# A hybrid gMLP / state-space block: first loads in smaller pieces, the norm weight loaded apart, the first product in k order, one product on the un-normalised input

## The chip, the cores and the metric

The kernel runs on one core of one Trainium2 chip. The metric is the time of one execution on the device, in microseconds (us), as the median of several runs. The engines named below are PE (TensorE, the matmuls), DVE (VectorE), ACT (ScalarE), POOL (GpSimd) and SP (SyncE, which here only issues transfers). Each engine works through its own list of instructions in order; an instruction that waits holds back everything behind it on that engine.

## The reference

One layer works on 512 tokens of 1024 channels, all in float32 (inputs and outputs). Cut to what matters here:

```python
xn   = rmsnorm(x, mix_norm_w)                       # x * rsqrt(mean(x^2)) * w
proj = xn @ w_in                                    # 1024 -> 9248 columns
g_a, g_b, za, z, xbc, dt_raw = split(proj)
y_a  = gmlp_mixer(za) @ w_proj_a
xbc  = silu(causal_dwconv(xbc, conv_w, conv_b))     # 4 taps; x, B, C channels
y_b  = ssd_scan(x, softplus(dt_raw + dt_bias), -exp(a_log), B, C) ... @ w_proj_b
h    = x + (sigmoid(g_a) * y_a + sigmoid(g_b) * y_b) @ w_out
h    = h + ConvGLU(rmsnorm(h))                      # 2816 wide, 3 taps
out  = rmsnorm(h)
```

The row factor rsqrt(mean(x^2)) of the first norm belongs to a token. A product of weights with x * w (without that factor) can therefore be multiplied by the factor afterwards, token by token.

## The kernel before, in words

**Tiles.** Activations lie with channels on the 128 partitions and the 512 tokens along the free axis: `xT0` to `xT7` are the eight tiles of x. To get float32 accuracy from the fast matmul type, every operand is split into a high part and a low part (`h` and `l` at the end of a name: `xw0h`, `xw0l`), and each product is three matmuls, hi·xh, hi·xl and lo·xh, each 128x128 by 128x512. `cols()` makes a pair of 128-column products (tiles `...p`, one PSUM bank each) from eight input tiles: the weights come in two k blocks of four tiles (`w0`, `w1`), and a pair is 48 matmuls. `weights()` loads a block (tag `wraw`, four buffers), ACT copies it to the high part and DVE subtracts to get the low part.

**Two versions of the input.** `xw` is x times the norm weight, without the row factor; it needs only `xT` and the norm weight. `xn` is the normalised input; it needs `rb`, the row factors in all partitions, which come from the squares of all x tiles (`xq`, token sums `xss` and the broadcast `rbp` on PE). The first two pairs, `B0` and `C0`, are made from `xw`, and `unnorm()` multiplies their results by `rb` afterwards (`B0u`, `C0u`); all later products of the projection use `xn`.

**Order of the stages on PE.** Thirteen small float32 matmuls on a tile of ones (`warm`), each of which shows as two records; then the pairs B0, C0 (with `xss`, the dt products `dtp` and `rbp` in the middle of C0), x0, x2, x4, x6, B2, C2, x8, x10, x12, x14, then the gMLP products, the z pairs, and the projections, up to the down projection `dn`. Four PSUM banks in two pairs take the results in turn: B0, x0, x4, B2, x8 and x12 use one pair of banks, C0, x2, x6, C2 and x10 the other. `conv()` reads a product straight out of its bank: one ACT pass and three DVE passes (widths 511, 510, 509); after the last of these the bank is free for the next pair but one.

**The chain of the time steps.** `dt_chain()` turns `dtp` into step sizes in five pieces, which are put between the stages at the places `CHAIN` gives. Its last pieces are the running sums `acp` (PE), their copy `ac_k` (ACT), the transposes `ach` (PE), and then `achs` and `eahs` (ACT), which are written to DRAM (`acum_d`, `ea_d`) and read back by `ssm_load()` as `s0bc` and so on; the first state-space steps begin with x8. `alog`, a 128x32 tile, is loaded on the POOL queue and exponentiated by ACT (an instruction of the first piece of that chain, which depends on nothing but its load).

**What sets the order.** PE's order follows the program for B0 and C0 by hand; everywhere else a list scheduler with a time model arranges the instructions of each engine when the kernel is built. So a change in one place can move instructions elsewhere.

Of the kernel before, what the change touches and what calls it, by code (L numbers as in the profile page):

```python
# [17 lines left out]
KD = D // P  # L18
# [10 lines left out]
R_MIX, R_GB, R_CB, R_NW, R_FN, R_FCB, R_FW, R_CW, R_FCW, R_D, R_LW, R_LB, R_ALL = 0, 8, 24, 48, 64, 72, 116, 124, 220, 352, 368, 376, 384  # L29
U_GA, U_GB, U_U, U_Z, U_XS, U_B, U_C = 0, 4, 8, 12, 20, 28, 30  # L30
# [3 lines left out]
def kernel(  # L34
# [6 lines left out]
    dve, act, pe, pool, sync = nc.vector, nc.scalar, nc.tensor, nc.gpsimd, nc.sync  # L41

    const = ctx.enter_context(tc.tile_pool(name="const", bufs=1))
# [6 lines left out]
    def T(name, dt=F32):  # L50
        return tp.tile([P, S], dt, tag="t", name=name)

    def PM(name):
        return pp.tile([P, S], F32, tag="mm", name=name, bufs=4)

    def PA(name):
        return pp.tile([P, S], F32, tag="aux", name=name, bufs=4)
# [4 lines left out]
    def f(t):  # L62
        return t.bitcast(F32)
# [10 lines left out]
    def weights(src, shape, name):  # L74

        pieces = [slice(None)]
        if ahead:
            raw = ahead.pop(0)
            pieces = [slice(0, 2), slice(2, 4)]
        else:  # L80
            raw = wp.tile(shape, F32, tag="wraw", name=name + "r", bufs=4)
            sync.dma_start(out=raw, in_=src)
        hi = wp.tile(shape, F32R, tag="whi", name=name + "h")
        lo = wp.tile(shape, F32R, tag="wlo", name=name + "l")
        for q in pieces:
            act.activation(out=hi[:, q], in_=raw[:, q], func=AF.Copy)
            dve.tensor_tensor(out=lo[:, q], in0=raw[:, q], in1=f(hi)[:, q], op=ALU.subtract)
        return hi, lo

    def cols(w, u, xs, name):  # L90

        K = len(xs)
        ps = [PM(f"{name}p{i}") for i in range(2)]
        nb = K // 4
        for kb in range(nb):
            hi, lo = weights(w[u, kb], [P, 4, 2 * P], f"{name}w{kb}")

            def mm(i, k, part):
                xh, xl = xs[4 * kb + k]
                c = slice(i * P, (i + 1) * P)  # L100
                if part == 0:
                    pe.matmul(ps[i], lhsT=hi[:, k, c], rhs=xh, start=(kb == 0 and k == 0), stop=False)  # L102
                    pe.matmul(ps[i], lhsT=hi[:, k, c], rhs=xl, start=False, stop=False)
                else:
                    pe.matmul(ps[i], lhsT=lo[:, k, c], rhs=xh, start=False, stop=(kb == nb - 1 and k == 3))  # L105

            if kb < nb - 1:
                order = [(i, k, part) for part in range(2) for k in range(4) for i in range(2)]
            else:
                order = [(i, k, part) for i in range(2) for part in range(2) for k in range(4)]  # L110
            for o in order:
                mm(*o)
            tick()
        return ps
# [4 lines left out]
    def defer(fn, n=1):  # L119
        later.append([n, fn])  # L120

    def tick():
        due = []
        for e in list(later):
            e[0] -= 1
            if e[0] <= 0:
                later.remove(e)
                due.append(e[1])
        for fn in due:
            fn()  # L130
# [4 lines left out]
    warm = PA("warm")  # L135
    for i in range(WARM):
        pe.matmul(warm[:, 0:P], lhsT=ones, rhs=ones, start=True, stop=True)  # L137
# [9 lines left out]

    one = const.tile([P, 1], F32, name="one")
    dve.memset(one, 1.0)
    pcol = const.tile([P, R_ALL], F32, name="pcol")  # L150
    act.dma_start(out=pcol, in_=cols_in)
    act.activation(out=one, in_=one, func=AF.Square)
    wdt = const.tile([P, KD, HEADS], F32, name="wdt")
    pool.dma_start(out=wdt, in_=wdt_in)
# [3 lines left out]
    pool.dma_start(out=alog, in_=alog_in[0].partition_broadcast(P))  # L158
    xT, ahead = [], []
    for k in range(KD):  # L160
        t = T(f"xT{k}")
        sync.dma_start(out=t, in_=xt_in[:, k, :])
        xT.append(t)
        if k % 4 == 0:
            raw = wp.tile([P, 4, 2 * P], F32, tag="wraw", name=f"first{k}", bufs=4)
            for q in range(0, 4, 2):
                sync.dma_start(out=raw[:, q:q + 2, :], in_=w_in[U_B, k // 4][:, q:q + 2, :])
            ahead.append(raw)

    def pc(r):  # L170
        return pcol[:, r:r + 1]


    def rstd(ssq, n, name):

        m = ssq.shape[-1]
        v = sm.tile([P, m], F32, tag="rsv", name=name + "v")
        dve.tensor_scalar(out=v, in0=ssq, scalar1=1.0 / n, scalar2=EPS, op0=ALU.mult, op1=ALU.add)  # L178
        r = sm.tile([P, m], F32, tag="rsr", name=name + "r")
        pool.tensor_tensor(out=r, in0=v, in1=mhalf[:, :m], op=ALU.pow)  # L180
        return r

    def token_sums(sq, name):

        ps = PA(name)
        n = sq.shape[-1] // P
        for c in range(n):
            pe.matmul(ps[:, c * P:(c + 1) * P], lhsT=sq[:, c * P:(c + 1) * P], rhs=ones, start=True, stop=True)  # L188
        return ps.rearrange("p (c t) -> p c t", t=P)[:, 0:n, 0]

    def bcast_tokens(r, name):

        ps = PA(name)
        n = r.shape[-1]
        for c in range(n):
            pe.matmul(ps[:, c * P:(c + 1) * P], lhsT=r[:, c:c + 1].to_broadcast([P, P]), rhs=ident,
                      start=True, stop=True)
        return ps[:, 0:n * P]


    xw = []
    for k in range(KD):
        h = T(f"xw{k}h", F32R)
        act.activation(out=h, in_=xT[k], func=AF.Copy, scale=pc(R_MIX + k))
        l = T(f"xw{k}l", F32R)
        dve.scalar_tensor_tensor(out=l, in0=xT[k], scalar=pc(R_MIX + k), in1=f(h), op0=ALU.mult, op1=ALU.subtract)
        xw.append((h, l))


# [1 line left out]
    for b in range(2):  # L211
        t = tp.tile([P, 4, P], F32R, tag="t", name=f"wdt{b}")
# [16 lines left out]
    xn = []  # L229
# [13 lines left out]
    def dt_product(b):  # L243
        for k in range(4 * b, 4 * b + 4):
            for i in range(2):
                pe.matmul(dtp, lhsT=wd2[b][:, k % 4, :], rhs=xw[k][i], start=(k == 0 and i == 0),
                          stop=(k == KD - 1 and i == 1))
# [71 lines left out]
    def conv(u, t, name):  # L319

        c = T(name)
        act.activation(out=c, in_=u, func=AF.Identity, scale=pc(R_CW + 72 + t), bias=pc(R_CB + t))
        for j in (1, 2, 3):
            dve.scalar_tensor_tensor(out=c[:, j:], in0=u[:, :S - j], scalar=pc(R_CW + 24 * (3 - j) + t),  # L324
                                     in1=c[:, j:], op0=ALU.mult, op1=ALU.add)
        act.activation(out=c, in_=c, func=AF.Silu)  # L326
        return c
# [130 lines left out]


    def conv_pair(u, ct, dst, i, name):  # L460
        ps = cols(w_in, u + i // 2, xn, name)
        for q in range(2):
            dst[i + q] = conv(ps[q], ct + i + q, f"{name}c{q}")

    with tc.manual_schedule(engines={mybir.EngineType.PE}):
        ps = cols(w_in, U_B, xw, "B0")

        def x_norm():
            r1 = rstd(token_sums(xacc, "xss"), D, "xr")
            dt_product(0)  # L470
            dt_product(1)
            act.copy(out=rb, in_=bcast_tokens(r1, "rbp"))
            us.extend(unnorm(ps[q], f"B0u{q}") for q in range(2))
            x_split()

        us = []
        defer(x_norm)
        psC = cols(w_in, U_C, xw, "C0")
# [22 lines left out]
    for b in range(2):  # L501
        ps = [PM(f"vp{b}{t}") for t in range(NT)]
# [12 lines left out]
        for t in range(NT):  # L515
# [19 lines left out]
    for i in range(0, 8, 2):  # L535
        ssm_step()
        ps = cols(w_in, U_U + i // 2, xn, f"u{i}")
        for q in range(2):
# [5 lines left out]
            for t in range(NT):  # L544
# [4 lines left out]
                                     in1=radd[b][:, gg:gg + P].unsqueeze(1).to_broadcast([P, NT, P]),  # L549
                                     op0=ALU.mult, op1=ALU.add)  # L550
# [43 lines left out]
    for i in range(0, 8, 2):  # L594
        ps = cols(wpa_in, i // 2, ya, f"pa{i}")
        for q in range(2):
            t = T(f"m{i + q}")
            act.copy(out=t, in_=ps[q])
            m.append(t)
    for i in range(0, 8, 2):  # L600
        for q in range(4):
            defer(lambda t=2 * i + q: y_split(t), 1 + q // 2)
        ps = cols(w_in, U_GA + i // 2, xn, f"ga{i}")
# [5 lines left out]
    for i in range(0, 8, 2):  # L609
        ps = cols(w_in, U_GB + i // 2, xn, f"gb{i}")  # L610
# [5 lines left out]
    for i in range(0, 8, 2):  # L616
        ps = cols(wpb_in, i // 2, yb, f"pb{i}")
# [8 lines left out]
    for i in range(0, 8, 2):  # L626
        ps = cols(wo_in, i // 2, ms, f"wo{i}")
        for q in range(2):
            k = i + q
            h = T(f"hT{k}")  # L630
# [53 lines left out]
    for i in range(NFF):  # L684
        ps = cols(wup_in, i, hs, f"up{i}")
# [53 lines left out]
T_BUFS = 74  # L739
XPOOL = (4, 6)  # L740
CHAIN = (1, 5, 9, 10)
WARM = 13


# [49 lines left out]
```

## Time and profile before

| what | value |
|---|---|
| time, median of 3 runs | 1041.57 us (1040.82 to 1041.67) |
| profiled execution, its own time | 1039.9 us |
| its span, first to last instruction | 1038.2 us |
| mean granted TensorE clock | 0.996 |
| PE busy | 1016.6 us (98%) |
| DVE / ACT / POOL busy | 616.6 (59%) / 451.2 (43%) / 52.6 (5%) us |
| bytes moved | 109.85 MB, mean 106 GB/s |

In a timeline row the first number is the start in us from the start of the span, the second the duration (of the whole group where the row ends in x2 or more), then engine, line, operation, the tile written, the arrow and the tiles read. What stands in brackets is idle time of the engine just ahead of the row, and what ended it. DMA rows give the tile, the queue that issued, the size and the time from issue to landing.

### The profile page before, as it was taken

The numbers are of one execution on the slowest core, as the hardware profiler recorded it, in microseconds if no ns is written. First come the engines' busy times: TensorE is split into PE (matmuls) and PEld (weight loads), VectorE is DVE, ScalarE is ACT, GpSimd is POOL, SyncE is SP. The second block draws the span as 40 slices with busy tenths as digits, with TensorE's granted clock in tenths as the row PEclk, the third lists the DMA queues.
The fourth block names the chain that finished last, engine by engine and source line by source line (L and its number), as shares of the span: only waits on it lengthen the run. The fifth ranks groups of instructions, "written<-read, shape, count | busy, mean of one in ns | idle before, by whom it ended". The sixth has DMA issues, their size and how long they took to land.

```text
span 1038.2 us, 12494 instructions
## 1 busy us (share of the span) xinstructions
PE 1016.6 (98%) x4858; PEld 840.3 (81%) x4858; DVE 616.6 (59%) x1002; ACT 451.2 (43%) x612; POOL 52.6 (5%) x77
## 2 busy tenths in 40 slices
PE   8999999999999988999999999999999999999996
PEld 7788887888888777888888888888888888888885
DVE  5886997878784654245223445567668677742124
ACT  7365874674564333244332224345444444422212
POOL 3100000220000100000000000000000000000003
PEclk9999999999999999999999999999999999999999
DMA  6333635424343223332233223332222323323302
GB/s 237 122 101 94 196 113 175 130 92 143 107 118 102 71 92 92 112 101 87 96 102 102 93 90 102 102 102 102 83 100 90 98 98 102 102 83 100 102 21 81
DMA packets 38205, 109.85 MB, mean 106 GB/s; under 512 B 6401, under 2 KB 6561, under 8 KB 38145
## 3 DMA queue, kind: packets, MB, share of 16 engines
q1 hardware_dynamic: 37312, 107.64, 32.2%
q10 hardware_dynamic: 720, 1.25, 0.3%
q8 instruction: 38, 0.62, 0.2%
q0 software_dynamic: 112, 0.16, 0.1%
q14 instruction: 23, 0.18, 0.1%
HBM read 106.79 MB, written 2.24 MB: 105 GB/s over the span
## 4 chain that ended last, share of the span: by engine, by line
PE 86%; DVE 3%; DMA 3%; issue 2%; POOL 1%; ACT 1%; POOLq 0%; DVEq 0%; SPq 0%
PE dn L702 10%; PE vp L509 1%; PE vp L511 1%; PE vp L510 1%; DMA yr_d<-yr1r 1%; DMA yrb<-yr_d 1%; DMA yr_d<-yr2r 1%; PE pb6p L102 1%; PE pb4p L102 1%; PE pb2p L102 1%; PE pb0p L102 1%; PE pb6p L105 1%; PE pb4p L105 1%; PE pb2p L105 1%; PE pb0p L105 1%
## 5 line engine op out<-in xcount | busy, mean ns | idle before, releaser
L722 POOL TENSOR_TENSOR htok<-htok,fnw 128x512 f32<-128x512 f32 x5 | 6.6, 1325 | 344.6 <-ACT fj L720 344.6
L378 ACT ACT_TABLE_LOAD x15 | 19.2, 1283 | 3.5 <-DMA s15bc<-acum_d 1.7
L180 POOL TENSOR_TENSOR hrr<-hrv,mhalf 128x4 f32<-128x4 f32 x1 | 1.0, 1007 | 261.0 <-DVE hrv L178 261.0
L633 ACT ACTIVATE hh<-hT,pcol 128x512 fp32r<-128x512 f32 x8 | 5.8, 725 | 15.0 <-DVE hT L631 15.0
L720 ACT ACTIVATE fj<-htok 128x512 f32<-128x512 f32 x8 | 5.0, 629 | 16.2 <-DVE htok L718 16.2
L188 PE MATMUL yss<-ones,yq 128*128 128x128 f32 x32 | 5.3, 319 | 6.6 <-DVE yq L588 6.6
L188 PEld LDWEIGHTS yss<-ones,yq 128*128 128x128 f32 x32 | 4.8, 225 | 7.7 <-issue 4.2
L588 DVE TENSOR_TENSOR yq<-yq,zs 128x512 f32<-128x512 f32 x12 | 8.4, 697 | 4.2 <-ACT zs L587 4.2
L607 DVE TENSOR_TENSOR m<-m,sa 128x512 f32<-128x512 f32 x8 | 5.5, 688 | 8.6 <-ACT sa L606 8.6
L326 ACT ACT_TABLE_LOAD x8 | 10.3, 1283 | 0.8 <-DVE C2c L324 0.7
L718 DVE TENSOR_TENSOR htok<-dn,htok 128x512 f32<-128x512 f32 x8 | 5.4, 686 | 7.1 <-PE dn L702 7.1
L566 DVE SCALAR_TENSOR_TENSOR x4c<-x4c,pcol,yrb 128x512 f32<-128x512 f32 x2 | 1.4, 749 | 11.9 <-DMA yrb<-yr_d 11.9
L545 PEld LDWEIGHTS sp<-wsT,v 128*128 128x128 f32 x64 | 7.8, 191 | 0.3
L635 DVE SCALAR_TENSOR_TENSOR hl<-hT,pcol,hh 128x512 fp32r<-128x512 f32 x8 | 6.0, 749 | 3.2 <-ACT hh L633 3.2
L235 DVE SCALAR_TENSOR_TENSOR xn<-xT,pcol,rb 128x512 f32<-128x512 f32 x8 | 7.8, 1005 | 0.0
L545 PE MATMUL sp<-wsT,v 128*128 128x128 f32 x64 | 7.8, 275 | 0.0
L566 DVE SCALAR_TENSOR_TENSOR x8c<-x8c,pcol,yrb 128x512 f32<-128x512 f32 x2 | 1.4, 747 | 10.3 <-DMA yrb<-yr_d 10.3
L521 DVE BATCH_NORM_STATS2 bst<-v 128x6 f32<-128x128 f32 x32 | 7.1, 282 | 0.3
L566 DVE SCALAR_TENSOR_TENSOR x12c<-x12c,pcol,yrb 128x512 f32<-128x512 f32 x2 | 1.4, 747 | 9.4 <-DMA yrb<-yr_d 9.4
L587 ACT ACTIVATE zs<-x8c 128x512 f32<-128x512 f32 x1 | 0.6, 636 | 14.5 <-DVE x8c L582 14.5
L566 DVE SCALAR_TENSOR_TENSOR x0c<-x0c,pcol,yrb 128x512 f32<-128x512 f32 x2 | 1.4, 747 | 8.5 <-DMA yrb<-yr_d 8.5
L137 PE MATMUL warm<-ones 128*128 128x128 f32 x26 | 5.4, 397 | 1.1 <-POOL ones L134 1.1
(4027 smaller groups left out, 3526.1 us busy)
## 6 DMA issues: line engine op xcount, KB each, us to landing
xT<-in_xt_dram SPq DMA_DIRECT2D x8, 256.0 KB, 6.6
first<-in_w_in_dram SPq DMA_DIRECT2D x4, 256.0 KB, 5.8
yrb<-yr_d SPq DMA_DIRECT2D x4, 256.0 KB, 5.1
out_dram<-htok ACTq DMA_DIRECT2D x4, 256.0 KB, 2.1
out_dram<-htok SPq DMA_DIRECT2D x4, 256.0 KB, 2.1
C0w0r<-in_w_in_dram SPq DMA_DIRECT2D x1, 512.0 KB, 6.0
C0w1r<-in_w_in_dram SPq DMA_DIRECT2D x1, 512.0 KB, 6.6
x0w0r<-in_w_in_dram SPq DMA_DIRECT2D x1, 512.0 KB, 7.1
```

The source lines that it names most:

```text
L102: pe.matmul(ps[i], lhsT=hi[:, k, c], rhs=xh, start=(kb == 0 and k == 0), stop=False)
L105: pe.matmul(ps[i], lhsT=lo[:, k, c], rhs=xh, start=False, stop=(kb == nb - 1 and k == 3))
L188: pe.matmul(ps[:, c * P:(c + 1) * P], lhsT=sq[:, c * P:(c + 1) * P], rhs=ones, start=True, stop=True)
L235: dve.scalar_tensor_tensor(out=n, in0=xT[k], scalar=pc(R_MIX + k), in1=rb, op0=ALU.mult, op1=ALU.mult)
L326: act.activation(out=c, in_=c, func=AF.Silu)
L378: act.activation(out=bc, in_=bc, func=AF.Exp)
L509: pe.matmul(ps[t], lhsT=xh[:, ts], rhs=hi[:, k, :], start=(kb == 0 and k == 0), stop=False)
L510: pe.matmul(ps[t], lhsT=xl[:, ts], rhs=hi[:, k, :], start=False, stop=False)
L511: pe.matmul(ps[t], lhsT=xh[:, ts], rhs=lo[:, k, :], start=False, stop=(kb == 3 and k == 1))
L545: pe.matmul(sp[:, t * P:(t + 1) * P], lhsT=vn[t][b][:, gg:gg + P], rhs=wsT[b][:, gg:gg + P], start=True, stop=True)
L588: dve.tensor_tensor(out=acc, in0=acc, in1=zs, op=ALU.add)
L702: pe.matmul(po[t][b], lhsT=l[:, ts], rhs=r[:, cs], start=(k == 0 and l is xh and r is hi), stop=(k == NFF - 1 and r is lo))
```

## The change

It makes six edits. The first k block of the B0 weights is loaded in four pieces of one k tile (128 KB) instead of two of two, each issued behind its x tile on SP; the x tile `xT1` is issued on ACT's queue. The eight columns of the norm weight are loaded alone (`pmix`, 4 KB) on ACT's queue, and the whole table of columns (`pcol`, 192 KB) goes to POOL's queue behind `alog`. `xw` reads `pmix`. B0's matmuls go k tile by k tile (hi·xh and hi·xl for both columns, then lo·xh for both). The pair x0 is made from `xw`, and two `unnorm()` multiplies make `x0u0` and `x0u1` from it ahead of the conv. The warm loop has 8 turns instead of 13.

```diff
         if ahead:
-            raw = ahead.pop(0)
-            pieces = [slice(0, 2), slice(2, 4)]
+            raw, pieces = ahead.pop(0)
...
-    def cols(w, u, xs, name):
+    def cols(w, u, xs, name, early=False):
...
-            if kb < nb - 1:
+            if early:
+                order = [(i, k, part) for k in range(4) for part in range(2) for i in range(2)]
+            elif kb < nb - 1:
...
+    pmix = const.tile([P, KD], F32, name="pmix")
+    act.dma_start(out=pmix, in_=cols_in[:, R_MIX:R_MIX + KD])
     pcol = const.tile([P, R_ALL], F32, name="pcol")
-    act.dma_start(out=pcol, in_=cols_in)
...
     for k in range(KD):
-        t = T(f"xT{k}")
-        sync.dma_start(out=t, in_=xt_in[:, k, :])
-        xT.append(t)
         if k % 4 == 0:
             raw = wp.tile([P, 4, 2 * P], F32, tag="wraw", name=f"first{k}", bufs=4)
-            for q in range(0, 4, 2):
-                sync.dma_start(out=raw[:, q:q + 2, :], in_=w_in[U_B, k // 4][:, q:q + 2, :])
-            ahead.append(raw)
+            parts = [slice(q, q + 1) for q in range(4)] if k == 0 else [slice(0, 2), slice(2, 4)]
+            ahead.append((raw, parts))
+        t = T(f"xT{k}")
+        (sync, act)[k % 2 if k < 2 else 0].dma_start(out=t, in_=xt_in[:, k, :])
+        xT.append(t)
+        for q in ahead[-1][1]:
+            if q.start == k % 4:
+                sync.dma_start(out=raw[:, q, :], in_=w_in[U_B, k // 4][:, q, :])
+    pool.dma_start(out=pcol, in_=cols_in)
...
-        act.activation(out=h, in_=xT[k], func=AF.Copy, scale=pc(R_MIX + k))
+        act.activation(out=h, in_=xT[k], func=AF.Copy, scale=pmix[:, k:k + 1])
...
     def conv_pair(u, ct, dst, i, name):
-        ps = cols(w_in, u + i // 2, xn, name)
+        first = name == "x0"
+        ps = cols(w_in, u + i // 2, xw if first else xn, name)
+        if first:
+            ps = [unnorm(ps[q], f"x0u{q}") for q in range(2)]
...
-        ps = cols(w_in, U_B, xw, "B0")
+        ps = cols(w_in, U_B, xw, "B0", early=True)
...
-WARM = 13
+WARM = 8
```

The scheduler answers with another order on several engines. Three places matter below.

**ACT, the start of the program.** `first` is the raw B0 weight block, `B0w0h` its high part, `alog` the little tile of the dt chain. Before:

```order
L151 DMA pcol<-in_cols_dram 128x384
L152 ACT_TABLE_LOAD
L152 ACTIVATE one<-one 128x1
L86 ACTIVATE B0w0h<-first_111 128x512 x2
L204 ACTIVATE xw0h<-xT_109,pcol 128x512
L204 ACTIVATE xw1h<-xT_114,pcol 128x512
L204 ACTIVATE xw2h<-xT_116,pcol 128x512
L275 ACTIVATE alog<-alog 128x32
```

With the change:

```order
L152 DMA pmix<-in_cols_dram 128x8
L154 ACT_TABLE_LOAD
L154 ACTIVATE one<-one 128x1
L168 DMA xT_109<-in_xt_dram 128x512
L85 ACTIVATE B0w0h<-first_105 128x256 x3
L280 ACTIVATE alog<-alog 128x32
L85 ACTIVATE B0w0h<-first_105 128x256
L209 ACTIVATE xw0h<-xT_106,pmix 128x512
```

`alog` stood behind `xw2h` and now stands ahead of the fourth weight piece and of `xw0h`.

**PE, from the transposes `ach` to x8.** Before, `ach` stands behind 22 of the 48 matmuls of C2:

```order
L105 MATMUL C2p_864<-xn2h,C2w0l 128x512
L105 MATMUL C2p_865<-xn2h,C2w0l 128x512
L303 MATMUL ach<-ident,ac_k 32x128 x4
L105 MATMUL C2p_864<-xn3h,C2w0l 128x512
L105 MATMUL C2p_865<-xn3h,C2w0l 128x512
```

and 26 more, the 12 small matmuls and transposes of `btp`, `cbp` and `s0xt`, and x8 follow. With the change:

```order
L102 MATMUL C2p_872<-xn6l,C2w1h 128x512
L308 MATMUL ach<-ident,ac_k 32x128 x4
L101 MATMUL C2p_872<-xn7h,C2w1h 128x512
L102 MATMUL C2p_872<-xn7l,C2w1h 128x512
L104 MATMUL C2p_872<-xn4h,C2w1l 128x512
L104 MATMUL C2p_872<-xn5h,C2w1l 128x512
L104 MATMUL C2p_872<-xn6h,C2w1l 128x512
L104 MATMUL C2p_872<-xn7h,C2w1l 128x512
L344 MATMUL btp_952<-ident,B0c_599 128x128 x4
L350 MATMUL cbp_959<-C0c_605,B0c_599 128x128 x4
L370 MATMUL s0xt<-ident,x0c_513 128x128 x4
L101 MATMUL x8p_987<-xn0h,x8w0h 128x512
```

`ach` now stands behind 42 of the 48, with six behind it. On ACT, `achs`, `eahs` and the first conv passes of B2 (`B2c`) follow `ach` in the same order in both kernels.

**DVE, the conv of B2.** Its passes free the banks that x8 takes. Before:

```order
L87 TENSOR_TENSOR x10w0l<-x10w0r,x10w0h 128x1024
L324 SCALAR_TENSOR_TENSOR B2c_845<-B2p_767,pcol,B2c_845 128x511
L324 SCALAR_TENSOR_TENSOR B2c_851<-B2p_768,pcol,B2c_851 128x511
L324 SCALAR_TENSOR_TENSOR B2c_845<-B2p_767,pcol,B2c_845 128x510
L324 SCALAR_TENSOR_TENSOR B2c_851<-B2p_768,pcol,B2c_851 128x510
L324 SCALAR_TENSOR_TENSOR B2c_845<-B2p_767,pcol,B2c_845 128x509
L324 SCALAR_TENSOR_TENSOR C2c_926<-C2p_864,pcol,C2c_926 128x511
L324 SCALAR_TENSOR_TENSOR B2c_851<-B2p_768,pcol,B2c_851 128x509
```

With the change:

```order
L329 SCALAR_TENSOR_TENSOR B2c_852<-B2p_774,pcol,B2c_852 128x511
L329 SCALAR_TENSOR_TENSOR B2c_858<-B2p_775,pcol,B2c_858 128x511
L329 SCALAR_TENSOR_TENSOR B2c_852<-B2p_774,pcol,B2c_852 128x510
L329 SCALAR_TENSOR_TENSOR B2c_858<-B2p_775,pcol,B2c_858 128x510
L86 TENSOR_TENSOR x10w1l<-x10w1r,x10w1h 128x1024
L381 TENSOR_SCALAR s0bc_864<-s0bc_864,ac_k 128x128 x3
L329 SCALAR_TENSOR_TENSOR B2c_852<-B2p_774,pcol,B2c_852 128x509
L329 SCALAR_TENSOR_TENSOR C2c_933<-C2p_871,pcol,C2c_933 128x511
```

The last pass of the first bank (width 509) now stands behind a weight split and behind three passes over `s0bc`, which is read back from DRAM.

More of the change, by code (lines that the diff above doesn't have):

```diff
@@ L203 @@
         h = T(f"xw{k}h", F32R)
-        act.activation(out=h, in_=xT[k], func=AF.Copy, scale=pc(R_MIX + k))
+        act.activation(out=h, in_=xT[k], func=AF.Copy, scale=pmix[:, k:k + 1])
         l = T(f"xw{k}l", F32R)
-        dve.scalar_tensor_tensor(out=l, in0=xT[k], scalar=pc(R_MIX + k), in1=f(h), op0=ALU.mult, op1=ALU.subtract)
+        dve.scalar_tensor_tensor(out=l, in0=xT[k], scalar=pmix[:, k:k + 1], in1=f(h), op0=ALU.mult, op1=ALU.subtract)
         xw.append((h, l))
```

## The prediction

> **What bounds the kernel now.** I read the page's first two parts first, then PE's timeline at the start and at the places where the change moves work, then ACT's and DVE's there.
>
> ```profile
> span 1038.2 us, 12494 instructions
> PE 1016.6 (98%) x4858; PEld 840.3 (81%) x4858; DVE 616.6 (59%) x1002; ACT 451.2 (43%) x612; POOL 52.6 (5%) x77
> PEclk9999999999999999999999999999999999999999
> ```
>
> PE is busy 98% of the span at full clock, so the time moves with when PE starts, where it waits, and at which clock it works. The profiled execution took 1039.9 us, 1.7 over its span and 1.67 under the median of 1041.57; I make the sum in its rows and carry it over by adding 1.67.
>
> The start, from PE's and ACT's timelines, POOL's issue of `alog`, and the DMA view (size, us from issue to landing):
>
> ```profile
> 1.05 5.35 PE L137 MATMUL warm<-ones 128*128 128x128 f32 x26 [1.05 <-POOL ones L134]
> 7.55 0.50 PE L102 MATMUL B0p<-xw0h,B0w0h 128*128 128x512 f32 x1 [1.14 <-ACT xw0h L204]
> 8.34 0.50 PE L103 MATMUL B0p<-xw0l,B0w0h 128*128 128x512 f32 x1 [0.29 <-DVE xw0l L206]
> 20.46 0.39 PE L105 MATMUL B0p<-xw7h,B0w1l 128*128 128x512 f32 x1
> 20.68 0.39 PE L102 MATMUL C0p<-xw0h,C0w0h 128*128 128x512 f32 x1
> ```
> ```profile
> 5.36 0.63 ACT L86 ACTIVATE B0w0h<-first 128x512 fp32r<-128x512 f32 x1 [2.62 <-DMA first<-in_w_in_dram]
> 6.79 0.71 ACT L204 ACTIVATE xw0h<-xT,pcol 128x512 fp32r<-128x512 f32 x1
> 9.90 0.72 ACT L204 ACTIVATE xw2h<-xT,pcol 128x512 fp32r<-128x512 f32 x1 [0.65 <-DMA xT<-in_xt_dram]
> 10.53 0.21 ACT L275 ACTIVATE alog<-alog 128x32 f32<-128x32 f32 x1
> 10.65 0.71 ACT L204 ACTIVATE xw3h<-xT,pcol 128x512 fp32r<-128x512 f32 x1
> ```
> ```profile
> 3.05 0.56 POOL L158 DMA_DIRECT2D alog<-in_alog_dram  x1
> ```
> ```profile
> xT<-in_xt_dram SPq DMA_DIRECT2D x8, 256.0 KB, 6.6
> first<-in_w_in_dram SPq DMA_DIRECT2D x4, 256.0 KB, 5.8
> wdt<-in_wdt_dram POOLq DMA_DIRECT2D x1, 128.0 KB, 5.0
> alog<-in_alog_dram POOLq DMA_DIRECT2D x1, 16.0 KB, 6.8
> ```
>
> The first product waits for `xw0h`, which waits for weights and x. The 24 matmuls of C0 from 20.68 to `xss` at 26.13 (a row below) give the pitch at full rate, 0.227 us; a pair of 48 is 10.9.
>
> **T1, the first product starts later: +3.6.** ACT is in order, and four quarter copies, the exponential of `alog`, and only then `xw0h` stand there. Two landings hold it. `alog` is issued on POOL behind the same transfers as before: 3.05 + 6.8 = 9.85. The fourth weight piece has ahead of it on SP four x tiles less `xT1` and three pieces: up to and with itself 3 x 256 + 4 x 128 = 1280 KB, exactly the bytes up to and with `xT2` before, which released `xw2h` at 9.90. So ACT goes on at about 9.9: exponential 0.12 (pitch 10.53 to 10.65), a quarter copy about 0.35 (half the tile of the 0.63 row, with some fixed part), `xw0h` 0.71; PE starts at 11.1 against 7.55. Bounds: with `alog` landing like `wdt`, 5.0 after issue, and the piece as early, 8.05, the start is 9.25 (+1.7); with both 0.6 late it is 11.7 (+4.2). I take the landings that the rows show. `alog` before stood behind `xw2h`, where its landing cost nothing.
>
> **T2, B0 itself runs closer: -1.7.** Before, B0 took 20.68 - 7.55 = 13.13, which is 2.23 over 10.9: waits for x tiles one after another. When it starts at 11.1 nearly all has landed, ACT makes a tile in about 0.62 to 0.7, and PE needs six matmuls, 1.36 us, per k tile. What is left is one wait for `xw0l`, which took 8.34 - 7.55 = 0.79, less one matmul 0.23: 0.56. 2.23 - 0.56 = 1.67. Bounds -1.2 to -2.2. With tiles this late the k order buys nothing more.
>
> **T3, the clock at the start: +2.0.** Eight warm turns are 16 records of 5.35 / 26 = 0.206 us: they end at 1.05 + 3.3 = 4.35, and PE idles 6.8 us. What a stop of 3.76 us does stands later in this trace (PE's timeline, then the windows view: from:to, length, busy time and count of PE, PEld, DVE, ACT, POOL, then granted clock, DMA share, GB/s):
>
> ```profile
> 408.99 2.04 PE L188 MATMUL yss<-ones,yq 128*128 128x128 f32 x8 [3.76 <-DVE yq L588]
> ```
> ```profile
> 405.30:408.40 3.10, 0.00 (x0) 0.00 (x0) 2.15 (x4) 1.69 (x4) 0.00 (x0) 1.00 0.24 54
> 408.50:411.80 3.30, 2.81 (x11) 2.64 (x12) 1.74 (x3) 0.57 (x1) 0.48 (x1) 0.50 0.43 143
> 411.90:413.00 1.10, 1.10 (x6) 0.89 (x6) 0.00 (x0) 0.00 (x0) 0.42 (x1) 1.00 0.94 369
> ```
>
> After that stop the granted clock was 0.50 until between 411.8 and 411.9: 2.85 us of work at half rate, 1.4 lost. The warm row shows another length: its records, 0.206 us each, are twice as long as those of `xss`, the same shape (the pitch below: 8 in 26.93 - 26.13, 0.10), so all 5.35 us of it went at half rate, where the column reads full; a start like that loses 2.7. I take the middle, 2.0. Zero would need a stop of 6.8 us to leave the clock alone where 3.76 didn't. Before, the gap ahead of the first product was 1.14.
>
> ```profile
> 26.13 1.05 PE L188 MATMUL xss<-ones,xq 128*128 128x128 f32 x8
> 26.93 0.48 PE L246 MATMUL dtp<-xw0h,wdt 128*128 128x512 f32 x1
> ```
>
> The Trainium skill, "TensorE: Matmul & The Clock Gate", "What's actually happening", says that the array is at half rate by default, falls back after an idle window of about 3.4 us and is released by a busy one, in windows that run freely. It speaks against a shorter warm-up followed by a longer gap; one window at half rate would make this term 1.7 and the sum 0.3 less. The trace agrees on the fall, and its warm row lasted longer than one window.
>
> **T4, x0 from `xw`: -1.9.**
>
> ```profile
> 37.02 0.61 PE L102 MATMUL x0p<-xn0h,x0w0h 128*128 128x512 f32 x2
> 46.62 0.50 PE L103 MATMUL x0p<-xn6l,x0w1h 128*128 128x512 f32 x1 [1.10 <-DVE xn6l L70]
> 49.95 0.39 PE L102 MATMUL x2p<-xn0h,x2w0h 128*128 128x512 f32 x1
> ```
> ```profile
> 47.09 1.28 DVE L316 TENSOR_TENSOR C0u<-C0p,rb 128x512 f32<-128x512 f32 x2
> 53.93 0.29 DVE L271 TENSOR_TENSOR dttmp<-dttok,dtb 128x128 f32<-128x128 f32 x1 [2.32 <-PE dttok L267]
> ```
>
> x0 took 49.95 - 37.02 = 12.93, 2.03 over 10.9: it waits for `xn` tiles as DVE makes them. `xw` is long there. The next one late is x2, whose bank `C0u` frees: its first multiply ends at 47.09 + 0.64 = 47.73 on the same footing where x2 could start at 37.02 + 10.9 = 47.92. So the gain is nearly whole; bounds -1.4 to -2.0. The two `x0u` multiplies, 1.28 us at the rate of the `C0u` row, fall where DVE idles 2.32 us (the last row); without that cover they would delay x0's conv by 1.28, and x4, which takes its banks a whole pair later, not at all.
>
> **T5, x8 waits for its bank: +4.1.**
>
> ```profile
> 94.08 0.40 PE L102 MATMUL C2p<-xn0h,C2w0h 128*128 128x512 f32 x1
> 94.68 0.48 PE L103 MATMUL C2p<-xn0l,C2w0h 128*128 128x512 f32 x1
> 99.54 0.60 PE L303 MATMUL ach<-ident,ac_k 128*32 128x128 f32 x4
> 105.92 0.60 PE L339 MATMUL btp<-ident,B0c 128*128 128x128 f32 x4
> 107.61 0.48 PE L102 MATMUL x8p<-xn0h,x8w0h 128*128 128x512 f32 x1
> ```
> ```profile
> 100.17 0.58 ACT L306 COPY achs<-ach 32x512 f32<-32x512 f32 x1 [0.73 <-PE ach L303]
> 101.14 1.42 ACT L322 ACTIVATE B2c<-B2p,pcol 128x512 f32<-128x512 f32 x2
> ```
> ```profile
> 101.94 3.38 DVE L324 SCALAR_TENSOR_TENSOR B2c<-B2p,pcol,B2c 128x511 f32<-128x511 f32 x5
> 106.61 0.88 DVE L376 TENSOR_SCALAR s0bc<-s0bc,ac_k 128x128 f32<-128x128 f32 x4
> 109.74 1.22 DVE L87 TENSOR_TENSOR x10w1l<-x10w1r,x10w1h 128x1024 fp32r<-128x1024 f32 x1
> 110.88 0.69 DVE L347 TENSOR_TENSOR cbm<-cbp,tri 128x512 f32<-128x512 f32 x1
> ```
>
> Before, the fifth B2 pass, the one that frees the first bank, ended at 101.94 + 3.38 = 105.3, and x8 began at 107.61: 2.3 to spare. All of it hangs on `ach`, since ACT's B2 passes stand behind `achs`. In the change `ach` has 42 matmuls of C2 ahead of it instead of 22. Counted in the times of before, with C2 1.9 earlier by T4 (a shift of everything, T1 to T3, changes no wait): C2 from 92.18, 42 x 0.227 = 9.55, `acp` 0.36 (94.08 to 94.68 less a matmul): `ach` from 102.1 to 102.7. Then PE has six matmuls, 1.36, and `btp` to `s0xt`, 107.61 - 105.92 = 1.69: ready for x8 at 105.75. The chain: to ACT's first B2 pass 0.97 (100.17 to 101.14), that pass 0.73: 104.4. DVE: four passes at 3.38 / 5 = 0.68, less overlap, 2.65: 107.05; the `x10w1l` split 1.14 (109.74 to 110.88): 108.2; three `s0bc` passes, 0.66, which need `s0bc` back from DRAM (before it was there at 106.61, at most 6.4 behind `achs`: here 109.1 at the latest): 108.85 to 109.75; the 509 pass 0.74: bank free between 109.6 and 110.5. PE waits 3.9 to 4.8; I take 4.1, because `s0bc` waited for nothing before and so lands earlier than that bound. Bounds 3.0 (DVE finds the split done before) to 5.0. Behind the waiting x8 stand all of PE's later products. The second bank is freed later still, but PE has 22 matmuls, 5.0 us, of the first column ahead of it.
>
> **At nothing:** `pcol` on POOL's queue lands by about 12 (as `alog`, and some more for its bytes); its first reader, `xn`, comes after the token sums, 26.13 and later; without that cover each us late is a us for x2. The two more issues on SP and the one more on ACT hide behind transfers that take 5.8 to 6.6 us to land. `pmix` is smaller than anything that lands there and is issued first; late, it would hold `xw0h` only past 10.4.
>
> **Sum:** 3.6 - 1.7 + 2.0 - 1.9 + 4.1 = +6.1: 1046.0 in the profiled execution, 1047.7 as a median.
>
> **Rivals.**
> - *D, the wait at x8 drops the clock too.* 4.1 us is over the 3.76 that did it; a loss of 1.4 to 2.0 more: 1049.4. Against it: one such stop in this trace is no rule, and the wait may be nearer to its lower bound. Chance 0.18. The page's rule of an idle window would have it so whenever a window falls inside the wait.
> - *B, no wait at x8*, if the ACT passes of B2 or DVE's split come sooner than counted: 6.1 - 4.1 = +2.0, 1043.6. For it: it is a count over ten instructions. Against: each is in order. Chance 0.13.
> - *A, faster:* ACT isn't held. If `alog` and the fourth piece land by 7, the start is 8.2 (+0.6); the gap then is 3.9, the clock may hold, B0 still gains 1.7 and x0 1.9, and x8 doesn't wait: -3.0, 1038.6. It decides at a landing of `alog` before about 8, against the row's 9.85. Chance 0.07.
> - *C, as A, but x8 waits:* +1.1, 1042.7. Chance 0.05.
> - The forecast: 0.57.
>
> **Numbers.** 0.2%, 2.1 us, is about what a measurement of this kernel can tell from no change. Faster is A and a little of C: 0.08. Within 0.2% are C and half of B: 0.13. Slower is the rest, 0.79. The likeliest time is 1047.7; its own terms, at bounds that don't all fall together, give 1045.5 to 1049.5; for B and D the range is 1043.5 to 1050.0.
>
> **What would show it.** T1: the first `B0p` released by `xw0h` near 11, with ACT's `alog` row behind a DMA wait and the fourth quarter copy after it. T2: B0 without waits of over 0.6. T3: a granted clock of 0.5, or matmuls of 0.45, at the start of B0. T4: x0 to x2 in 10.9, no `xn` releaser. T5: `x8p` with about 4 us of wait on DVE's `B2c`. Wrong I am if `alog` lands early, if PE starts before 9, or if x8 follows `s0xt` without a wait.

## The result and the profile after

The changed kernel takes 1047.27 us as a median (1045.88 to 1049.85, five runs) against 1040.82 us for the kernel before (1036.74 to 1041.67, five runs). The ratio, taken of the means (1047.51 to 1039.74), is 1.0075, 95% interval 1.0047 to 1.0102. It is slower, by 6.5 us in the medians and 7.8 in the means; predicted were 6.1. The profiled execution took 1047.27 us, with a span of 1045.6 against 1038.2, 7.4 longer.

From the page of the changed kernel:

```profile
span 1045.6 us, 12484 instructions
PE 1019.4 (98%) x4848; PEld 844.5 (81%) x4848; DVE 618.5 (59%) x1006; ACT 447.6 (43%) x612; POOL 53.8 (5%) x78
```

and the three longest waits of PE in the view of waits (in all, times, longest):

```profile
PE B0p L101 <- ACT xw0h L209: 5.8, 1, 5.8
PE yss L193 <- DVE yq L596: 4.8, 2, 2.8
PE x8p L101 <- DVE B2c L329: 3.9, 1, 3.9
```

The first was 1.1 before and the third is new, and they are the two the prediction named. PE is still busy 98%: the slower matmuls at half rate count as busy, so the page's share hides them.

**The start**, from ACT's timeline, PE's timeline and the DMA view of the changed kernel:

```profile
7.82 0.42 ACT L85 ACTIVATE B0w0h<-first 128x256 fp32r<-128x256 f32 x1 [1.38 <-DMA first<-in_w_in_dram]
8.62 0.23 ACT L280 ACTIVATE alog<-alog 128x32 f32<-128x32 f32 x1 [0.38 <-DMA alog<-in_alog_dram]
9.53 0.42 ACT L85 ACTIVATE B0w0h<-first 128x256 fp32r<-128x256 f32 x1 [0.68 <-DMA first<-in_w_in_dram]
9.85 0.71 ACT L209 ACTIVATE xw0h<-xT,pmix 128x512 fp32r<-128x512 f32 x1
```
```profile
1.05 3.78 PE L138 MATMUL warm<-ones 128*128 128x128 f32 x16 [1.05 <-POOL ones L135]
10.61 0.80 PE L101 MATMUL B0p<-xw0h,B0w0h 128*128 128x512 f32 x1 [5.77 <-ACT xw0h L209]
...
16.25 0.63 PE L101 MATMUL B0p<-xw2h,B0w0h 128*128 128x512 f32 x1
16.68 0.50 PE L102 MATMUL B0p<-xw2l,B0w0h 128*128 128x512 f32 x1
17.02 0.39 PE L101 MATMUL B0p<-xw2h,B0w0h 128*128 128x512 f32 x1
```
```profile
alog<-in_alog_dram POOLq DMA_DIRECT2D x1, 16.0 KB, 5.5
```

The last six warm records, in the changed kernel and then in the kernel before, from PE's timeline of a narrow window:

```profile
3.35 1.49 PE L138 MATMUL warm<-ones 128*128 128x128 f32 x6
```
```profile
5.48 0.92 PE L137 MATMUL warm<-ones 128*128 128x128 f32 x6
```

ACT waits for the third piece, for `alog`, for the fourth piece, and only then makes `xw0h`. `alog` landed at 8.6, earlier than before; the fourth piece at 9.5 came last. PE starts at 10.61, after an idle stretch of 5.77, and its matmuls start 0.43 apart until 16.7, and 0.23 apart from 17.0 on: the first 6 us of B0 go at half rate. The clock had not come up before that: the warm records of the changed kernel start 0.21 apart to the last one, while in the kernel before the last of them start 0.11 apart. C0 starts at 24.77, 4.09 later than before.

**x0 and x8**, from PE's and DVE's timelines and the windows view (granted clock in the third column from the end):

```profile
41.11 0.39 PE L101 MATMUL x0p<-xw0h,x0w0h 128*128 128x512 f32 x1
52.18 0.47 PE L101 MATMUL x2p<-xn0h,x2w0h 128*128 128x512 f32 x1
106.41 0.60 PE L308 MATMUL ach<-ident,ac_k 128*32 128x128 f32 x4
114.05 0.77 PE L101 MATMUL x8p<-xn0h,x8w0h 128*128 128x512 f32 x1 [3.89 <-DVE B2c L329]
```
```profile
108.80 2.73 DVE L329 SCALAR_TENSOR_TENSOR B2c<-B2p,pcol,B2c 128x511 f32<-128x511 f32 x4 [3.43 <-ACT B2c L327]
111.44 1.22 DVE L86 TENSOR_TENSOR x10w1l<-x10w1r,x10w1h 128x1024 fp32r<-128x1024 f32 x1
112.58 0.67 DVE L381 TENSOR_SCALAR s0bc<-s0bc,ac_k 128x128 f32<-128x128 f32 x3
113.16 0.74 DVE L329 SCALAR_TENSOR_TENSOR B2c<-B2p,pcol,B2c 128x509 f32<-128x509 f32 x1
```
```profile
114.00:119.00 5.00, 4.95 (x12) 3.92 (x13) 5.00 (x14) 4.94 (x5) 0.00 (x0) 0.50 0.75 243
119.50:124.00 4.50, 4.50 (x21) 3.69 (x20) 4.50 (x12) 3.64 (x6) 0.00 (x0) 1.00 0.44 136
```

x0 takes 11.07 and waits for nothing. x8 waits 3.89 on the 509-wide pass of B2, which stands behind the split and the `s0bc` passes, just as counted. Then x8 runs its first 5 us at a granted clock of 0.5.

How much later than before PE reaches each place (the start of the first matmul of a tile, after less before):

| place | before | after | later by | what happened since the row above |
|---|---|---|---|---|
| B0 | 7.55 | 10.61 | 3.06 | `xw0h` behind the fourth piece |
| C0 | 20.68 | 24.77 | 4.09 | B0: fewer waits (-1.55), half rate (+2.58), told apart by e5 below |
| x2 | 49.95 | 52.18 | 2.23 | x0 without waits (-1.9) |
| C2 | 94.08 | 96.41 | 2.33 | |
| x8 | 107.61 | 114.05 | 6.44 | wait for B2's bank (+4.1) |
| x10 | 119.61 | 128.52 | 8.91 | x8 at half rate (+2.5) |
| v products | 159.06 | 167.29 | 8.23 | |
| dn | 909.15 | 916.75 | 7.60 | small gains in later waits |

Of the 8.9 at x10, 1.3 comes back by `dn`, in several small steps; the waits for `yss` are one of them (4.8 in all, 6.6 before). I didn't follow up the others.

### The profile page after: what moved, and what is told of

Its sections match the earlier page's. It is cut to its first block, busy times and chain, and to the rows that moved or that the text cites. A ratio compares the mean times of both kernels' runs of the same rounds, so it can differ in the third digit from the quotient of the medians.

```text
span 1045.6 us, 12484 instructions
## 1 busy us (share of the span) xinstructions
PE 1019.4 (98%) x4848; PEld 844.5 (81%) x4848; DVE 618.5 (59%) x1006; ACT 447.6 (43%) x612; POOL 53.8 (5%) x78
## 4 chain that ended last, share of the span: by engine, by line
PE 89%; DVE 3%; DMA 3%; issue 2%; ACT 1%; POOL 1%; POOLq 0%; DVEq 0%; SPq 0%
PE dn L710 10%; PE vp L517 1%; PE vp L519 1%; PE vp L518 1%; DMA yr_d<-yr2r 1%; DMA yr_d<-yr1r 1%; PE pb6p L101 1%; PE pb4p L101 1%; PE pb2p L101 1%; PE pb0p L101 1%; PE pb6p L104 1%; PE pb4p L104 1%; PE pb2p L104 1%; PE pb0p L104 1%; PE pb6p L102 1%
```

## The experiments

### First set: start and x0 apart, and the place of `ach`

Theory: the change is two parts that don't touch each other. The start edits cost what stands at C0; the x0 edit gains 1.9 at x0, and moves `acp` and `ach` on PE, which brings the wait at x8. The rival is that the wait at x8 belongs to the start edits.

**e1, only the x0 edit on the kernel before:**

```diff
-        ps = cols(w_in, u + i // 2, xn, name)
+        first = name == "x0"
+        ps = cols(w_in, u + i // 2, xw if first else xn, name)
+        if first:
+            ps = [unnorm(ps[q], f"x0u{q}") for q in range(2)]
```

> The kernel before, with only the x0 pair made from xw (and its two x0u multiplies); loads, warm-up and B0 are as before. The scheduler then puts the transposes ach behind 42 matmuls of C2 here too, as in the whole change. Theory (the wait at x8 comes with the x0 edit, through the place of ach): C0 starts at 20.7 as before; x0 to x2 takes 11.0 instead of 12.9, so C2 starts 1.9 earlier; x8 waits about 3.9 us on DVE's B2c, so it starts 2 us later than before, and if the clock falls in that wait x8 loses up to 2.5 more; at the end 1.5 to 4 us slower than before. Rival (the wait at x8 comes from the start edits, through transfers that moved): no wait at x8, 1.9 us faster throughout.

Measured: ratio 1.0031 (1.0013 to 1.0049), slower. In the trace C0 starts 0.18 earlier than before, x2 1.93 earlier, x8 2.62 later and x10 4.15 later; the end of the span is 1.7 later. PE's timeline:

```profile
110.23 0.76 PE L102 MATMUL x8p<-xn0h,x8w0h 128*128 128x512 f32 x1 [4.23 <-DVE B2c L324]
```

The wait at x8 comes with the x0 edit alone, and so does the half clock behind it (x8 to x10 takes 13.53 against 12.00). An edit that takes two microseconds of waiting out of PE makes the kernel slower.

**e2, the change with x0 back on `xn`:**

```diff
-        first = name == "x0"
+        first = False
```

> The whole change with the x0 pair put back on xn; all edits of the start stay. ach stands behind 22 matmuls of C2 as before. Theory: first product near 10.6, B0 partly at half rate, C0 about 4.1 later than before, x0 waits for xn again (12.9), no wait at x8, at the end about 4 us slower than before, less what later waits give back. Rival (the wait at x8 comes from the start edits): a wait of about 4 at x8 and 8 us slower.

Measured: ratio 1.0035 (1.0020 to 1.0050), slower. First product at 10.57, C0 2.73 later than before, x8 2.75 later with no wait, and the end of the span 3.3 later. C0 is late by less than in the change, since B0 took 12.84 here and 14.16 there, at a start that was the same to 0.04: more on this at e5.

**e3, the x0 edit with `acp` and `ach` held near their old places:** every step of C2's loop but the first is ordered behind `acp`, and from the twelfth on behind `ach` (`place` holds the two instructions).

```diff
-            for o in order:
-                mm(*o)
+            for j, o in enumerate(order):
+                if name == "C2":
+                    n = j + (kb * len(order))
+                    with tc.issue_after(place["ach" if n >= 11 else "acp"]) if n else nullcontext():
+                        mm(*o)
+                else:
+                    mm(*o)
...
```

> The kernel before, with the x0 pair made from xw, and acp and ach held on PE near their old places (behind 2 and 19 matmuls of C2) by ordering C2's matmuls behind them; nothing else. Theory (the late ach is the cause of the wait at x8): x0 to x2 in 11.0, no wait at x8, about 1.9 us faster than before up to x8, and 1 to 2 at the end if the later waits on the state-space chain don't take it back. Rival (two more multiplies on DVE delay B2's conv, whatever the place of ach): x8 waits 2 us or more, and the end is no earlier than before.

Measured: ratio 0.9970 (0.9953 to 0.9987), faster than before. PE's timeline:

```profile
97.17 0.60 PE L309 MATMUL ach<-ident,ac_k 128*32 128x128 f32 x4
105.92 0.48 PE L102 MATMUL x8p<-xn0h,x8w0h 128*128 128x512 f32 x1
```

x8 starts 1.69 earlier than before with nothing waited for, and the gain is still there at the end (2.7 at `dn`). DVE has the same two extra multiplies as e1: they aren't the cause. The wait at x8 is the place of `ach`. Holding it also moved DVE's `x10w1l` split back behind the B2 passes, from its timeline:

```profile
103.80 0.87 DVE L382 TENSOR_SCALAR s0bc<-s0bc,ac_k 128x128 f32<-128x128 f32 x4 [0.91 <-DMA s0bc<-acum_d]
104.59 0.74 DVE L330 SCALAR_TENSOR_TENSOR B2c<-B2p,pcol,B2c 128x509 f32<-128x509 f32 x1
107.34 1.21 DVE L87 TENSOR_TENSOR x10w1l<-x10w1r,x10w1h 128x1024 fp32r<-128x1024 f32 x1
```

That move is not what removed the wait, by an estimate from these rows: the split (1.13 to the next row on DVE) ahead of `s0bc` would have filled the 0.91 of idle time there and delayed the 509 pass by 0.22, and its end at 105.33 is 0.59 ahead of x8.

**e4, the whole change with `ach` held the same way** (the diff of e3, on the changed kernel).

> The whole change, with acp and ach held on PE near their old places in C2 in the same way. Theory: the start as in the change (C0 4.1 later than before), x0 1.9 shorter, no wait at x8 and no half clock there, so about 2.2 later than before at x8 and 2 us slower at the end, 5 us faster than the change. Rival: the wait at x8 stays, and the time is that of the change.

Measured: ratio 1.0005 (0.9988 to 1.0022), the same as before and 0.7% under the change. x8 starts without a wait. C0 is 5.12 later than before, a little more than in the change, because the fourth piece landed later still (first product at 11.76), and x8 is 3.44 later. In the timed runs the two parts add up: the start costs what e2 shows, and the x0 edit, once `ach` is in place, gives back what e3 shows.

### Second set: what holds the start

**e5, the change with 30 warm turns:**

```diff
-WARM = 8
+WARM = 30
```

> The change with 30 warm turns (60 records) instead of 8, so that PE is busy until about 9 to 10 and not idle for 5.8 us ahead of the first product. Theory (the idle gap puts B0 at half rate): the first product stays near 10.6 to 11.7, B0 takes 10.9 to 11.5 instead of 12.8 to 14.2, and C0 starts 2 to 3 earlier than in the change; x8 still waits 3.9; 2 to 3 us faster than the change at the end. Rival (B0 is slow for another cause, its order by k tile or its tiles): B0 takes 13 to 14 here too.

Measured: ratio 1.0045 (1.0027 to 1.0063) to before. PE's timeline:

```profile
1.06 9.48 PE L138 MATMUL warm<-ones 128*128 128x128 f32 x60 [1.06 <-POOL ones L135]
11.01 0.51 PE L101 MATMUL B0p<-xw0h,B0w0h 128*128 128x512 f32 x1 [0.46 <-ACT xw0h L209]
...
22.59 0.39 PE L101 MATMUL C0p<-xw0h,C0w0h 128*128 128x512 f32 x1
```

The start is 0.4 later than in the change, B0 takes 11.58 instead of 14.16, and x2 starts where it does in the kernel before (50.00). So the half rate is what makes B0 slow, and it costs 2.6. The intervals of this kernel and of the change overlap, so the times alone would not have told it.

e5 takes away the idle gap and the short warm-up together, so it can't say which of them is the cause. The traces on record can. In the change the clock was not up when the warm-up ended (the row of 1.49 above), so the gap had nothing to drop. e7 and e8 below have the same 8 turns and gaps of only 1.71 and 1.62, and start at half rate too; e1, with 13 turns and a gap of 1.77, starts B0 at full rate. In e2, with 8 turns, the last six warm records took less, so the clock had come up, and there it fell in the gap; timeline and windows view of e2:

```profile
3.35 1.09 PE L138 MATMUL warm<-ones 128*128 128x128 f32 x6
```
```profile
7.40:10.50 3.10, 0.00 (x0) 0.00 (x0) 0.85 (x2) 1.66 (x5) 0.00 (x0) 0.50 0.96 348
14.20:17.20 3.00, 3.00 (x15) 2.49 (x14) 3.00 (x5) 3.00 (x5) 0.00 (x0) 1.00 1.00 397
```

So B0's half rate has two ways to come about, a warm-up that ends too early and a gap, and in the change's trace it was the first. Which of them it is differs between executions, since e2 and the change have the same warm-up. This is also why B0 took 12.84 in e2: there the clock was back at about 14.2, in the change at about 16.9.

**e6, ACT and DVE ordered by hand at the start**, piece k and `xw` of k in turn:

```diff
+    with tc.manual_schedule(engines={mybir.EngineType.Activation, mybir.EngineType.DVE}):
+        for k in range(KD):
...
+            for q in parts:
+                if q.start == k % 4:
+                    act.activation(out=hi[:, q], in_=raw[:, q], func=AF.Copy)
+            h = T(f"xw{k}h", F32R)
+            act.activation(out=h, in_=xT[k], func=AF.Copy, scale=pmix[:, k:k + 1])
+            l = T(f"xw{k}l", F32R)
+            dve.scalar_tensor_tensor(out=l, in0=xT[k], scalar=pmix[:, k:k + 1], in1=f(h), op0=ALU.mult, op1=ALU.subtract)
+            for q in parts:
+                if q.start == k % 4:
+                    dve.tensor_tensor(out=lo[:, q], in0=raw[:, q], in1=f(hi)[:, q], op=ALU.subtract)
...
```

> The change with ACT and DVE ordered by hand at the start: piece k, xw of k, piece k+1 and so on, so that only the first quarter of the weights stands ahead of xw0h; the exponential of alog still falls behind the first piece. Theory (whatever stands ahead of xw0h on ACT sets the start; in the change the fourth piece, landing at 9.5, and alog at 8.6): the first product starts right behind alog's landing, about 8.6 + 0.1 + 0.7 = 9.4, with a gap of 4.5 behind the warm-up and B0 at half rate at first; C0 1 earlier than in the change. Rival (the start is bound by the transfers of x and the norm weight): no earlier than 10.6.

Measured: ratio 1.0053 (1.0035 to 1.0070). ACT's timeline:

```profile
4.97 0.42 ACT L215 ACTIVATE B0w0h<-first 128x256 fp32r<-128x256 f32 x1 [2.22 <-DMA first<-in_w_in_dram]
9.35 0.23 ACT L291 ACTIVATE alog<-alog 128x32 f32<-128x32 f32 x1 [3.96 <-DMA alog<-in_alog_dram]
9.49 0.71 ACT L217 ACTIVATE xw0h<-xT,pmix 128x512 fp32r<-128x512 f32 x1
```

Now `alog` is the one that holds ACT, for 3.96 us, and the first product starts 0.89 behind its row, at 10.24. It starts right behind `alog` as the theory says; that `alog` landed 0.7 later here than in the change leaves little to see in the time of the start.

**e7, the same with `alog`'s exponential behind the last `xw` tile** (`last` is ACT's copy that makes it):

```diff
-        act.activation(out=alog, in_=alog, func=AF.Exp)
+        with tc.issue_after(last):
+            act.activation(out=alog, in_=alog, func=AF.Exp)
```

> As the run before, with the exponential of alog put behind the last xw tile. Theory: the first product starts about 1.1 behind the landing of the first piece, 5.3 + 0.4 + 0.7 = 6.4, only 1.6 behind the warm-up, so no fall of the clock; B0 then follows the landings of its tiles, each about 1 us after the other, and C0 starts between 17.5 and 18.5; the token sums xss may then wait for the squares on DVE, up to 2 us; x8 still waits 3.9. Rival (alog isn't what holds ACT): a start near 9.4 again.

Measured: ratio 1.0039 (1.0019 to 1.0058). PE's timeline:

```profile
6.56 0.79 PE L100 MATMUL B0p<-xw0h,B0w0h 128*128 128x512 f32 x1 [1.71 <-ACT xw0h L217]
...
19.39 0.39 PE L100 MATMUL C0p<-xw0h,C0w0h 128*128 128x512 f32 x1
...
26.62 1.16 PE L192 MATMUL xss<-ones,xq 128*128 128x128 f32 x8 [1.63 <-DVE xq L242]
```

The start is where the transfers allow it, at 6.56: the one small instruction had cost 3.7 us against e6. C0 misses my bounds (17.5 to 18.5): B0 took 12.83, its first 3.5 us at half rate, though I had expected none behind so short a gap. And the 1.3 us that C0 is ahead of the kernel before are lost at once, at `xss`, which waits 1.63 for DVE's last sum of squares and starts 0.5 later than before. x8 waits 3.9 here too.

**e8, the same with `ach` held** (the diff of e3 on top).

> As the run before, with acp and ach held near their old places in C2 as well. Theory: the start of that run, C0 2 to 3 earlier than in the kernel before, x0 1.9 shorter, no wait at x8: 3.5 to 5 us faster than before up to x8, less what xss waits, and 3 to 5 at the end if the later waits don't take it back. Rival (the later waits on the state-space chain are what bounds the end): no faster than the kernel before with x0 edited and ach placed, 2.7 in its trace.

Measured: ratio 0.9992 (0.9975 to 1.0008), the same as before. The first product starts at 6.45, but B0 took 14.25, 6.5 us of it at half rate, and C0 starts at 20.70, with the early start all used up. x2 is 1.15 earlier than before, against 1.80 in e3. My expectation of 3.5 to 5 was wrong; its rival, no faster than e3, came true in the time, but not in its cause: the gain was lost in B0 and at `xss` (0.37 of wait), not in the later waits on the state-space chain.

### Third set: keeping an early start

**e9, e8 with 13 warm turns:**

```diff
-WARM = 8
+WARM = 13
```

> The kernel with ACT ordered by hand, alog late and ach placed, with the warm-up back at 13 turns, so that it ends near 6.4, where the first product begins. Theory (in that kernel B0 ran 6 us at half rate, because the short warm-up stopped 1.6 us early, and the early start is then lost at xss, which waits for the squares): B0 in 11.2 to 12, C0 at 17.7 to 18.5, 2 to 3 earlier than before; but xss still not before 26.6, with a wait of about 3 for DVE's last sum of squares, so x2 at 48.7 and the time that of the run before. Rival (the start gain is kept): x2 2 to 3 earlier than 48.8 and 1034 in the trace.

Measured: ratio 0.9985 (0.9971 to 0.9998). C0 starts at 19.93, 0.75 earlier than before, and not at the 17.7 to 18.5 expected. No matmul of B0 goes at half rate here, and yet it takes 13.54, against 11.58 in e5. Two of its tiles come late: `xw3h` stands on ACT behind the fourth weight piece, which landed at 10.49 (1.1 us of B0), and `xw7h` behind C0's first weight block, which had to land (0.7 us):

```profile
10.49 0.42 ACT L221 ACTIVATE B0w0h<-first 128x256 fp32r<-128x256 f32 x1 [2.10 <-DMA first<-in_w_in_dram]
15.63 1.06 ACT L84 ACTIVATE C0w0h<-C0w0r 128x1024 fp32r<-128x1024 f32 x1 [0.64 <-DMA C0w0r<-in_w_in_dram]
16.60 0.70 ACT L223 ACTIVATE xw7h<-xT,pmix 128x512 fp32r<-128x512 f32 x1
```

`xss` waits 1.59 and starts at 27.12; x2 starts at 49.20, 0.75 earlier than before and later than e3's 48.15. As the theory has it, the early start is worth nothing at x2.

**e10, e9 with all sums of squares on DVE, ahead of the split of x0's weights:**

```diff
-    for eng, k0 in ((pool, 0), (dve, 4)):
-        for k in range(k0 + 1, k0 + 4):
-            eng.tensor_tensor(out=xq[k0], in0=xq[k0], in1=xq[k], op=ALU.add)
-    dve.tensor_tensor(out=xq[0], in0=xq[0], in1=xq[4], op=ALU.add)
+    for k in range(1, KD):
+        lastq = dve.tensor_tensor(out=xq[0], in0=xq[0], in1=xq[k], op=ALU.add).ins
+    hold["x0w0"] = lastq
...
```

`hold` makes the load and split of the block `x0w0` wait for the last sum.

> As the run before, with all seven sums of squares on DVE, right behind the squares, and ahead of the split of x0's weights (before, three were on POOL, and one such split stood ahead of the last sum). Theory (the last sum of squares is what holds the early start back): the last sum ends near 23.5, xss waits less than 0.7, x0 starts near 34.5 and x2 near 45.5, limited by the C0u multiplies behind xn on DVE; 4 to 5 earlier than the kernel before up to x8, and 3 to 5 at the end. Rival (what binds is the chain behind: xn on DVE, or later the state-space chain): x2 no earlier than 47.5, or the gain gone by the z pairs.

Measured: ratio 0.9969 (0.9953 to 0.9985), faster than before and no different from e3. `xss` starts at 25.10, 2 earlier than in e9, and x2 at 47.25, 2.70 earlier than before. The direction is the theory's; the size is between it and the rival, since the last sum ended at 25.0 and not at 23.5. In this one trace `dn` starts 6.6 earlier than before, but 1.8 of that comes between the pairs pa0 and pa2, around `yss`, where the clock held in this execution (`yss` took 1.13, against 2.04 in the kernel before); the timed runs show 3.

## Why the prediction was right, and where its sizes were off

The predicted median was 1047.7 and the measured one 1047.27. The terms, as the trace of the change has them:

| term | predicted | measured | what set it |
|---|---|---|---|
| T1, first product later | +3.6 | +3.06 | landing of the fourth piece, 9.5 |
| T2, B0 closer | -1.7 | -1.55 (by e5) | one wait for `xw0l` left |
| T3, half rate at the start | +2.0 | +2.58 (by e5) | 6 us at half rate |
| T4, x0 on `xw` | -1.9 | -1.86 | no `xn` wait, x2 0.2 late |
| T5, wait at x8 | +4.1 | +4.1 | `ach` late, DVE's order |
| D, half rate at x8 | a rival, +1.4 to +2.0 | +2.5 | the wait is an idle stretch |
| later waits | 0 | -1.3 to -1.5 | not followed up |

**T1** was right in its mechanism. I named two landings that come together at 9.9. In the run `alog` came at 8.6 and the fourth piece at 9.5, and the second decided; the exponential itself cost the change little. e6 and e7 show what it costs where the pieces don't hold ACT: 3.7 us.

**T2 and T3** can be told apart by e5, which starts B0 about as late and has no half rate in it. B0 took 11.58 there, 1.55 less than in the kernel before: T2, with the one wait for `xw0l` that the prediction left. The change's B0 took 2.58 more than that: T3, inside its bounds of 1.4 to 2.7. But the mechanism of T3 was only half right. I argued from a stop that drops the clock. In the change's trace the clock had not come up at all when the 8 turns ended, and the gap of 5.77 had nothing to drop; in e2's trace the gap did drop it. My reading that all 5.35 us of the warm row before went at half rate was off in the same place: its last records, 0.11 apart, are at full rate. That the middle of the two lengths I read there came near the measured size is luck in part.

**T4 and T5** hold to 0.1 or so. e1, e3 and e4 show the cause of T5: with `ach` near its old place the wait is gone, with the start edits and without, and with the x0 edit alone it is there.

**D** is where the forecast and the trace part. I took as likeliest that the clock holds through the wait at x8, and gave the fall 0.18. It fell in the change, and in e1, in waits of 3.9 and 4.2 us. The row I had quoted, a fall after 3.76, spoke for it, and I should have made it the likely case. That the total came out is luck in part: T3 and D were 3.1 too small together, T1 0.5 too large, and the later waits gave 1.3 to 1.5 back, which I had at nothing. In the rows the change cost 7.4, not 6.1. The medians agree to 0.4 because I added 1.67 for a profiled execution below its median, and the profiled execution of the change is its median.

The Trainium skill, "TensorE: Matmul & The Clock Gate", "What's actually happening", has windows of about 3.4 us that run freely. The traces agree in that starts 0.04 apart give different times at half rate: B0 took 14.16 in the change and 12.84 in e2. By it, as an estimate, a release takes between one and two windows of work, 3.4 to 6.8 us. From the first matmul on, the runs show 3.5 (e7), 6.3 (the change) and 6.5 (e8) in B0, but about 2.8 in the warm-up of e2, which is less than one. Behind the `yss` stop of the kernel before, the half clock lasted from about 408.4 to 411.9 by the prediction's windows, about one window; the 2.85 us that I took are only the part of it in which PE worked.

## What to carry to other kernels

Where a scheduler sets the order, an edit that removes a wait moves work far behind it: look at which instructions changed places on the engines ahead of the next bank or buffer, since that can cost twice the gain. On an engine that works in order, one small instruction that depends on a slow transfer, or a weight copy not needed yet, stands for the time of its landing in front of everything behind it. And count a wait of over 3.3 us on PE with the half-rate matmuls behind it, 1.4 to 2.5 us in these runs (`yss` before, x8 in e1 and in the change), and don't count on a shorter one to be free of them. A warm-up that can end before the clock is up doesn't protect the first product: the change lost 2.6 us there. An earlier start is worth nothing if the next stage waits for something that didn't move.

## What the runs showed of the hardware

The granted clock of the profile reads 1.00 at the start, where the matmuls go at half rate. In the changed kernel, windows view:

```profile
10.70:12.60 1.90, 1.90 (x4) 1.21 (x5) 1.90 (x4) 1.90 (x4) 0.00 (x0) 1.00 1.04 388
17.10:20.00 2.90, 2.90 (x14) 2.36 (x13) 2.35 (x3) 2.90 (x6) 1.09 (x1) 1.00 0.72 239
```

Four matmuls in 1.9 us and 14 in 2.9, both at a column of 1.00: at the start the pitch of the matmuls is to be read, not the clock.

How long a wait of PE must be for the clock to fall has no single answer in these twelve traces. Where the clock was up, all twelve waits of 3.3 us or more (3.31 to 7.16) brought a stretch at 0.50. Shorter waits went either way: it fell at the start of e3, with a gap of 1.90, and held at `yss` in e10, with one of 3.24. In e2 it fell at 348.6 with no single wait over 1.2, where PE had been busy 1.3 us of the 3.4 before (last row; from 348.7 to 352.0 the column reads 0.50). e3's windows view, e10's timeline, e2's windows view:

```profile
8.00:11.30 3.30, 3.16 (x8) 2.00 (x8) 2.35 (x4) 2.09 (x4) 0.00 (x0) 0.50 1.04 390
```
```profile
403.68 1.13 PE L203 MATMUL yss<-ones,yq 128*128 128x128 f32 x8 [3.24 <-DVE yq L618]
```
```profile
345.20:348.60 3.40, 1.33 (x11) 0.74 (x7) 3.11 (x8) 1.83 (x3) 1.25 (x1) 1.00 0.00 0
```

A stretch at 0.50 lasted about 3.4 us (x8 in e1) or 6.8 (x8 in the change, B0 in e2), once 10.2 (B0 in e4).

The sums of squares on DVE take 0.69 us each when POOL is quiet and up to 1.6 while POOL makes sums of its own. From the groups by form of tile `xq`, in the change and then in e10 (durations in ns: least, median, most):

```profile
L230 POOL TENSOR_TENSOR xq<-xq,xq x3: 1300/1627/1703, 18.9 to 22.1; 128x512 f32<-128x512 f32 x3
L230 DVE TENSOR_TENSOR xq<-xq,xq x3: 679/1597/1602, 20.9 to 24.6; 128x512 f32<-128x512 f32 x3
```
```profile
L251 DVE TENSOR_TENSOR xq<-xq,xq x7: 686/692/694, 19.2 to 24.4; 128x512 f32<-128x512 f32 x7
```

The Trainium skill, "GPSIMD Engine Reference", "1. Specifications", says that POOL shares its SBUF interfaces with DVE and that DVE instructions with two SBUF inputs contend for them; the rows agree. Seven sums on DVE alone (4.8 us) cost it little more than four beside POOL's three (0.68 twice and 1.60 twice, 4.6).
